# The mixer's c, v and b by seven block products in place of eight, with the state-space scan re-staged around them

## The chip, the cores and the metric

One Trainium2 chip, one of its cores. The metric is device time in microseconds (us) of one execution. Rows of the profile come from one profiled execution of the kernel before; times of runs come from three executions.

## The reference, cut to what matters

One decoder layer on x of 1024 tokens by 1024 features: a first SwiGLU feed-forward, the mixer, a second SwiGLU feed-forward, each behind an adaptive norm. The mixer is:

```python
h = modulate(rms_norm(x, mix_norm[l]), sh2, sc2)
proj = h @ w_in[l]
b_gate, c_gate, v, u = jnp.split(proj, [D_CONV, 2 * D_CONV, 3 * D_CONV], axis=-1)
y_conv = short_conv_mixer(b_gate, c_gate, v, conv_w[l])       # b * conv3_causal(c * v)
y_ssm = s5_mixer(u, ...)     # 32 groups of 16 channels, complex states scanned over time, GELU, GLU
y_mix = jnp.concatenate([rms_norm(y_conv, ...), rms_norm(y_ssm, ...)], axis=-1)
x = x + g2[:, None, :] * (y_mix @ w_out[l])
```

D_CONV is 512, so c, v and b are each a product of (1024 x 1024) by (1024 x 512), and u is a fourth of the same size.

## The kernel before, in words

**Products.** Features lie on partitions and tokens on the free axis, in two halves of 512 (`h` is 0 or 1). Every float32 operand is held as a high and a low fp32r part. `mm3` multiplies one 128-row piece of a weight tile by one 128x512 piece of an activation with three matmuls (high by high, high by low, low by high) and then calls `clock.tick()`. A projection of 128 output features over one half is eight `mm3`, 24 matmuls.

**Weights.** The class `Weights` streams raw weight tiles of 128x1024 float32 (512 KB) through three buffers by SP's DMA queue; ScalarE casts the high part (`CAST w<-raw`) and VectorE subtracts for the low part (`TENSOR_TENSOR w<-raw,w`). Four such pairs (`w`) exist at once. Where a block product needs a sum of weight blocks, GpSimd issues an accumulating DMA onto the raw tile (L175) after the earlier use of it.

**Seven products.** The feed-forwards already use `seven()` (L638): a 2x2 block product by seven instead of eight block multiplications, on combinations S1 to S4 of the activation's four blocks A11, A12, A21, A22. A group has a side "g" and a side "u"; each of its seven steps (`left`) is four `mm3` for either side, into three PSUM banks per side (A, B, C), with copies by ScalarE and sums by VectorE between. With the order `SOON` the first two steps are plain blocks of the first half, and the combinations are needed from the third step on. `combos3` (L597) makes S1 to S4 of the second feed-forward's input.

**The mixer before.** The norm h2 is followed by u: four weight tiles, 48 matmuls each for both halves, 192 in all. Its result `ya` goes to DRAM (`u_d`, 32 DMAs of 64 KB) in the scan's layout. Then, for i = 0 to 3, c_i is copied by ScalarE (`cs`), v_i is multiplied in by VectorE, and VectorE runs the three-tap convolution: one TENSOR_SCALAR and four SCALAR_TENSOR_TENSOR into `ya[i]`. Then b for both halves, multiplied into `ya`, the norm of it (`nAa`, `nAb`), the GLU (`gl`) and the output projection (`wo`). c, v and b are 12 weight tiles and 576 matmuls of 128x512.

**The scan.** It runs beside c, v and b in eight batches of four groups. `states(b)` (L1516) multiplies the input `ub` by `mi` on TensorE into `px`, copies it to `X`, sends it to `swx` with its two halves of partitions exchanged (two DMAs of 128 KB), and then on VectorE rotates (`co`, `si`), scans (four TENSOR_TENSOR_SCAN), rotates back, with a second exchange `swz`. `outputs(b)` (L1541) makes `yy` from `ub` by the Toeplitz matrix `mk` and from the states `co` by `mo`, takes the GELU (`yg`) and stores it (`y_d`). All these DMAs are issued by SP, in the order of the program.

**What sets the order.** `Clock` counts `mm3` calls; `clock.after(n, f)` runs `f` n ticks later, and each call that is due is written into the program there. A scheduler then orders each engine's instructions, and each engine executes its own in that order; a wait holds up everything behind it on the same engine. `states(b)` stands at tick 20 + 16b from the start of c, `outputs(b)` 22 ticks later (L1563, L1564). After the last batch, 32 DMAs bring `yb` back from `y_d`.

Of the kernel before, what the change touches and what calls it, by code (L numbers as in the profile page):

```python
# [21 lines left out]
P = 128  # L22
# [209 lines left out]
def hymba_layer(ctx: ExitStack, tc, x_d, xt_d, wm1_d, wmod_d, gu1_d, gs1_d, ds10_d, ds11_d, wl1_d, win_d, wout_d, glu_d, gu2_d, gs2_d, wd2_d, ds20_d, ds21_d, ds22_d, wl2_d, cols_d, cond_d, lam_d, bc_d, out_d):  # L232
# [70 lines left out]
    plain([win_d[i] for i in range(8)] + [glu_d] + [wout_d[i] for i in range(4)])  # L303
# [284 lines left out]
    lefts3 = {"S1": [], "S2": []}  # L588

    def copied3(k, h):  # L590

        left, i = {(1, 0): ("S1", 0), (1, 1): ("S1", 1), (0, 0): ("S2", 0), (0, 1): ("S2", 1)}[h, k // 4]
        if i == 0:
            lefts3[left].append(mov(f"h3{left}_{k}", dict(S1="B", S2="A")[left]))
        return lefts3[left][k % 4][:, i, :].bitcast(F32)

    def combos3(act):  # L597

        blocks.clear()
        while act[1] is None or len(act[1]) < KT:  # L600
# [3 lines left out]
        saved = scratch.tile([4, P, HALF], F32, name="s4_d")  # L604
# [7 lines left out]
        for k in range(4):  # L612
            s1, s3, s2, s4 = (t2k(f"h3w{i}_{k}")[:] for i in (1, 3, 2, 4))
            t1, t2 = (lefts3[left][k] for left in ("S1", "S2"))
# [7 lines left out]
            SP.dma_start(saved[k], s4)  # L622
            split_into("S2", t2, s2)
            yield
            split_into("S3", mov(f"h3S3_{k}"), s3)
            yield
        for k in range(4):
            t = mov(f"h3S4_{k}")
            hi, lo = t[:, 0, :], t[:, 1, :]
            SP.dma_start(lo.bitcast(F32), saved[k])  # L630
            split_into("S4", t, lo.bitcast(F32))
            yield
# [5 lines left out]
    def seven(name, between=None, kept=None, then=None, order=SEVEN):  # L638
# [11 lines left out]
        def out(side, h, fi, src, t):  # L650
            if side == "g":
# [8 lines left out]
        for n, (left, b) in enumerate(order):  # L660
            (w,) = ws.take()
            for half, side in enumerate("gu"):
# [22 lines left out]
                else:  # L685
                    if side == "g":
                        last = pools["first"].tile([P, HALF], F32, tag="first", name=f"{name}c21") if "first" in pools else acc_in_mov(f"{name}c21")
# [331 lines left out]
    u_d = scratch.tile([TAU, CH, G, J], F32, name="u_d")  # L1019
    y_d = scratch.tile([TAU, CH, G, J], F32, name="y_d")  # L1020
# [315 lines left out]
    def after1(d, h):  # L1336
        n2[h].add(x[d][h], beside=d < 6)
        if d == KT - 1:
            norm_into(act2, h, n2[h], 1, "h2")
# [20 lines left out]
    def fetch_last(left):  # L1360

        if left in ("A11", "A12", "A22"):
            i = ("A11", "A12", "A22").index(left)
            for h in range(2):
                for fi in range(2):
                    g, block = LAST[0][i], f"A{h + 1}{fi + 1}"
                    a_last[i][fi, h] = split_act(kept[g].of(block), f"fa{g}l{block}") if g else fetch(kept[g], block, "A", f"fa{g}l")

    back = [(h, k) for ks in ((0, 2), (1, 3)) for h in range(2) for k in ks]
# [5 lines left out]
    def x_back(left):  # L1375

        if left == "S4":
# [4 lines left out]
            open_x(ctx)  # L1382
# [37 lines left out]
    pools["acc"] = es2.enter_context(tc.tile_pool(name="accp", bufs=2))  # L1420
    yp = es2.enter_context(tc.tile_pool(name="yp", bufs=1))
    ya = [yp.tile([P, S], F32, tag=f"ya{i}", name=f"ya{i}") for i in range(4)]

# [6 lines left out]
    nA = [Sumsq("nAa"), Sumsq("nAb")]  # L1430
# [16 lines left out]
    def across(i, move, dram, t):  # L1447

        for g in range(8):
            move(  # L1450
                dram[:, :, 8 * i + g, :].rearrange("t c j -> c t j"), t[g * CH : (g + 1) * CH].rearrange("c (t j) -> c t j", t=TAU)
            )

    sp_open = ExitStack()
    sp = sp_open.enter_context(tc.tile_pool(name="sp", bufs=1))
    w4 = ws.take(4)
    for h in range(2):
        if h == 0:
            outs = [ps(f"u{i}_{h}") for i in range(4)]
            for k in range(KT):  # L1460
                ready(act2, h, k + 1)
                for w, o in zip(w4, outs):
                    mm3(o[:], w, k, act2[h][k], k == 0, k == KT - 1)
# [422 lines left out]
```

## Time and profile before

| what | value |
|---|---|
| three runs | 1688.48 us median, 1684.78 to 1691.4 |
| the profiled execution | 1685.48 us, of which the span from first to last instruction is 1683.7 us |
| granted TensorE clock, mean | 0.997 |
| busy: TensorE, VectorE, ScalarE, GpSimd | 98%, 64%, 41%, 10% of the span |
| u, in the span's own time | 693.8 to 741.9 us |
| c, v, b with the scan | 741.9 to 905.2 us |
| GLU, output projection | 905.2 to 937, 937 to 1040 us |

Times of rows are in us from the start of the span. A profiled execution is 1.78 us longer than its span, and this one lies 3.0 us under the median of the three runs. "PE" is TensorE's matmuls, "DVE" VectorE, "ACT" ScalarE, "POOL" GpSimd, "SPq" SP's queue of DMA issues. Busy times of neighbouring instructions overlap a little, since one starts while the last one drains.

### The profile page before, as it was taken

The numbers are of one execution on the slowest core, as the hardware profiler recorded it, in microseconds if no ns is written. First come the engines' busy times: TensorE is split into PE (matmuls) and PEld (weight loads), VectorE is DVE, ScalarE is ACT, GpSimd is POOL, SyncE is SP. The second block draws the span as 40 slices with busy tenths as digits, with TensorE's granted clock in tenths as the row PEclk, the third lists the DMA queues.
The fourth block names the chain that finished last, engine by engine and source line by source line (L and its number), as shares of the span: only waits on it lengthen the run. The fifth ranks groups of instructions, "written<-read, shape, count | busy, mean of one in ns | idle before, by whom it ended". The sixth has DMA issues, their size and how long they took to land.

```text
span 1683.7 us, 20572 instructions
## 1 busy us (share of the span) xinstructions
PE 1651.7 (98%) x7509; PEld 1360.4 (81%) x7509; DVE 1085.7 (64%) x1608; ACT 686.0 (41%) x1011; POOL 172.8 (10%) x211
## 2 busy tenths in 40 slices
PE   8999999999999999999999999999999999999998
PEld 5888888878878888788878778888888888888887
DVE  7984488869566768726556847856555555444576
ACT  6654333324455341332214416434444444322345
POOL 2010100101010102100000121000001011001004
PEclk9999999999999999999999999999999999999999
DMA  9476699989978667145653324557887777889732
GB/s 352 137 168 188 174 266 262 263 241 266 294 214 237 164 193 263 38 118 163 194 157 113 103 98 148 129 137 221 233 238 208 216 223 224 275 274 320 241 77 101
DMA packets 129272, 333.77 MB, mean 198 GB/s; under 512 B 17298, under 2 KB 41106, under 8 KB 128147
## 3 DMA queue, kind: packets, MB, share of 16 engines
q1 hardware_dynamic: 112466, 272.68, 46.7%
q0 software_dynamic: 16704, 59.78, 20.4%
q8 instruction: 59, 0.97, 0.2%
q14 instruction: 43, 0.34, 0.1%
HBM read 251.27 MB, written 72.74 MB: 192 GB/s over the span
## 4 chain that ended last, share of the span: by engine, by line
PE 83%; DVE 7%; DMA 7%; issue 2%; ACT 1%; POOL 1%; SPq 0%; DVEq 0%; POOLq 0%; ACTq 0%
PE fald L113 3%; PE fbd_1B L113 3%; PE fbd_0B L113 3%; PE p L113 3%; PE fad_0B L113 2%; PE fad_1B L113 2%; PE wo L113 2%; PE u L113 2%; PE b L113 2%; PE c L113 1%; PE fbd_1C L113 1%; PE fbd_0C L113 1%; PE v L113 1%; PE fb0d L113 1%; PE fad_0C L113 1%
## 5 line engine op out<-in xcount | busy, mean ns | idle before, releaser
L113 DVE TENSOR_TENSOR w<-raw,w 128x1024 fp32r<-128x1024 f32 (+1 forms) x247 | 298.7, 1211 | 255.1 <-ACT w L113 250.8
L113 ACT CAST w<-raw 128x1024 fp32r<-128x1024 f32 (+1 forms) x247 | 256.4, 1039 | 301.4 <-DMA raw<-in_ds 56.6
L175 POOL DMA_DIRECT2D raw<-in_gs x80 | 70.4, 883 | 737.0 <-DVE w L113 424.7
L113 DVE CUSTOM_DVE_ANT_0 wm<-wm,cact 128x1024 f32<-128x1024 f32 x56 | 76.4, 1378 | 12.9 <-DMA wm<-in_wmod 12.9
L175 POOL DMA_DIRECT2D raw<-in_ds x36 | 31.5, 875 | 312.6 <-DVE w L113 179.2
L113 PE MATMUL p<-h,w 128*128 128x512 f32 x192 | 49.4, 407 | 1.8 <-ACT h L113 1.5
L113 PE MATMUL wo<-oa,w 128*128 128x512 f32 x192 | 45.5, 391 | 2.4 <-ACT w L113 1.7
L113 PE MATMUL wo<-ob,w 128*128 128x512 f32 x192 | 45.7, 392 | 1.1 <-ACT ob L113 0.6
L113 PE MATMUL c<-h,w 128*128 128x512 f32 x192 | 46.0, 393 | 0.0
L113 PE MATMUL v<-h,w 128*128 128x512 f32 x192 | 46.0, 393 | 0.0
L113 PE MATMUL b<-h,w 128*128 128x512 f32 x192 | 45.1, 392 | 0.0
L113 PE MATMUL u<-h,w 128*128 128x512 f32 x192 | 44.8, 392 | 0.2 <-DVE h L113 0.2
L113 PEld LDWEIGHTS wo<-oa,w 128*128 128x128 f32 x192 | 35.8, 188 | 10.6 <-ACT w L113 2.1
L113 PEld LDWEIGHTS p<-h,w 128*128 128x128 f32 x192 | 35.7, 192 | 10.0 <-ACT h L113 2.0
L113 PEld LDWEIGHTS wo<-ob,w 128*128 128x128 f32 x192 | 35.7, 188 | 9.3 <-ACT ob L113 1.0
L113 PEld LDWEIGHTS u<-h,w 128*128 128x128 f32 x192 | 35.7, 188 | 8.3 <-DVE h L113 0.6
L113 PEld LDWEIGHTS b<-h,w 128*128 128x128 f32 x192 | 35.7, 188 | 7.3
L113 PEld LDWEIGHTS c<-h,w 128*128 128x128 f32 x192 | 35.5, 188 | 7.1
L113 PEld LDWEIGHTS v<-h,w 128*128 128x128 f32 x192 | 35.5, 188 | 7.1
L113 DVE TENSOR_TENSOR X<-co,X 128x512 f32<-128x512 f32 x8 | 5.5, 693 | 38.2 <-DMA swx<-X 34.6
L113 PE MATMUL fb0u<-h,w 128*128 128x512 f32 x96 | 23.8, 391 | 0.0
L113 PE MATMUL fb0g<-h,w 128*128 128x512 f32 x96 | 23.2, 389 | 0.0
(1558 smaller groups left out, 3874.9 us busy)
## 6 DMA issues: line engine op xcount, KB each, us to landing
raw<-in_gs SPq DMA_DIRECT2D x80, 512.0 KB, 4.9
raw<-in_gs POOLq DMA_DIRECT2D x80, 512.0 KB, 6.5
wm<-in_wmod SPq DMA_DIRECT2D x56, 512.0 KB, 6.2
raw<-in_ds SPq DMA_DIRECT2D x32, 512.0 KB, 4.9
raw<-in_ds POOLq DMA_DIRECT2D x32, 512.0 KB, 7.0
mw<-in_wm SPq DMA_DIRECT2D x8, 1024.0 KB, 8.7
raw<-in_win SPq DMA_DIRECT2D x16, 512.0 KB, 4.2
xb<-in_xt SPq DMA_DIRECT2D x8, 512.0 KB, 9.0
```

The source lines that it names most:

```text
L113: r = getattr(self.engine, name)(*args, **kw)
L175: self.G.dma_start(out=r, in_=src, accum_op=ALU.add)
```

## The change

c, v and b become three calls of `seven()`: `cv0` (c_0, c_1 as side g and v_0, v_1 as side u), `cv2` and `b`, all in the order `SOON`, 168 ticks in all. Their weights come as four blocks (`in_wcvb`), with 12 accumulating DMAs. `combos` makes S1 to S4 of h2, for which the norm h2 now leaves copies of its pieces (`copier`, 16 DMAs of 256 KB), and u's second half goes over four k for all four tiles first. The rows of x go to DRAM (`x_s`) and come back after the sevens. The scan is five steps per batch with 15 ticks between batches; `swx`, `swz`, `ub` and `y_d` are issued by ScalarE (`A.dma_start`); the product by `mk` is made in the first step into a PSUM tile of its own (`py`). The convolution's four taps are set two ticks apart, `yb` comes back tile by tile.

```diff
-    plain([win_d[i] for i in range(8)] + [glu_d] + [wout_d[i] for i in range(4)])
+    plain([win_d[i] for i in range(2)])
+    for i in range(3):
+        ws.seven(wcvb_d[i], soon=True)
+    plain([glu_d] + [wout_d[i] for i in range(4)])
...
-            norm_into(act2, h, n2[h], 1, "h2")
+            norm_into(act2, h, n2[h], 1, "h2", "A", copier(lefts2, "h2"))
...
+    clock.side.append(combos(act2, lefts2, "h2", "B", lambda: opened, lambda: u_free, s4_rest))
+    clock.period = 2
...
+    for k in range(4):
+        for w, o in zip(w4, outs):
+            mm3(o[:], w, k, act2[1][k], k == 0, False, more=True)
+    u_free.append(True)
...
+    def b_out(side, h, fi, src, t):
+        i = fi + 2 * (side == "u")
+        y = ya[i][:, hsl(h)]
+        joined(y, src[:], y, ALU.mult, fi == 1)
+        nA[h].add(y)
+        if nA[h].count == 4:
+            outnorm(actA, ya, nA[h], h, C_ONC, "oa", 8)
...
+    def u_load(b):
+        held["u", b] = sp.tile([P, GB, J], F32, tag="u", name=f"ub{b}", bufs=2)
+        A.dma_start(held["u", b][:], groups(u_d, b))
...
     def swapped(src, b, nm):
 
-        sw = sp.tile([P, GB * P], F32, tag="sw", name=f"{nm}{b}")
-        SP.dma_start(sw[0:64], src[64:128])
-        SP.dma_start(sw[64:128], src[0:64])
+        sw = sp.tile([P, GB * P], F32, tag=nm, name=f"{nm}{b}")
+        A.dma_start(sw[0:64], src[64:128])
+        A.dma_start(sw[64:128], src[0:64])
         return sw
...
+    def state_in(b):
+
+        u, mi, mk = (held.pop((n, b)) for n in ("u", "mi", "mk"))
         px = ps(f"px{b}")
+        py = held["py", b] = sm([P, GB * J], f"py{b}")
         for g in range(GB):
             q = slice(g * P, (g + 1) * P)
-            T.matmul(px[:, q], lhsT=held["mi"][:, q], rhs=u[:, g, :], start=True, stop=True)
+            T.matmul(px[:, q], lhsT=mi[:, q], rhs=u[:, g, :], start=True, stop=True)
+        X = held["X", b] = sp.tile([P, GB * J], F32, tag="sX", name=f"sX{b}")
+        A.copy(X[:], px[:])
+        held["sw", b] = swapped(X, b, "swx")
+        for g in range(GB):
+            q = slice(g * P, (g + 1) * P)
+            T.matmul(py[:, q], lhsT=mk[:, q], rhs=u[:, g, :], start=g == 0, stop=False, skip_group_check=True)
+        if b + 2 < NB:
+            u_load(b + 2)
...
+    STEPS = (0, state_in), (9, state_scan), (16, state_swap), (22, state_end), (27, outputs)
     for b in range(NB):
-        clock.after(20 + 16 * b, lambda b=b: states(b))
-        clock.after(20 + 16 * b + 22, lambda b=b: outputs(b))
+        for n, step in STEPS:
+            clock.after(6 + 15 * b + n, lambda b=b, step=step: step(b))
+    last = 6 + 15 * (NB - 1) + 27
     for i in range(4):
-        (w,) = ws.take()
-        cs = sp.tile([P, S], F32, tag="us", name=f"cs{i}")
+        clock.after((122, 128, 134, last + 1)[i], lambda i=i: y_back(i))
+    clock.after(last + 13, lambda: split_g(0))
+    clock.after(last + 22, lambda: split_g(1))
+    for i in range(0, 4, 2):
+        seven(f"cv{i}", order=SOON, emit=cv_out(i))
+    seven("b", order=SOON, emit=b_out)
```

**Place 1: batch 0's input product on TensorE, and ScalarE's queue ahead of it.** A number behind a name is the index of the batch, tile or weight; "x3" is one `mm3`. Before, `px0` stood behind all of c_0 and half of v_0:

```order
L113 MATMUL v0_0_6032<-h25_0_5578,w113_5865 128x512 x3
L113 MATMUL v0_0_6032<-h26_0_5586,w113_5865 128x512 x3
L113 MATMUL v0_0_6032<-h27_0_5594,w113_5865 128x512 x3
L113 MATMUL px0_6045<-ub0_5962,mi0_5956 128x128 x4
L113 MATMUL v0_1_6085<-h20_1_5706,w113_5865 128x512 x3
```

Now, on TensorE, six `mm3` after the end of u (four of `cv0gB`, then the first two rows here):

```order
L113 MATMUL cv0uB_6114<-h20_0_5546,w112_5973 128x512 x3
L113 MATMUL cv0uB_6114<-h21_0_5557,w112_5973 128x512 x3
L113 MATMUL px0_6121<-ub0_6087,mi0_6081 128x128 x4
L113 MATMUL py0_6122<-ub0_6087,mk0_6083 128x128 x4
L113 MATMUL cv0uB_6114<-h22_0_5574,w112_5973 128x512 x3
L113 MATMUL cv0uB_6114<-h23_0_5585,w112_5973 128x512 x3
L113 MATMUL cv0gA_6154<-h24_0_5596,w114_6036 128x512 x3
```

And ScalarE's queue around the end of u now, where before no DMA stood (raw70 holds the weights of w112, onto which the accumulating DMA adds before w115 is cast from it):

```order
L113 CAST w114_6036<-raw72_5641 128x1024
L113 COPY ya3_5669<-u3_1_5860 128x512
L113 CAST w115_6068<-raw70_5517 128x1024
L113 DMA ub0_6087<-u0_d_691 128x512
L113 COPY cv0gt1_6112<-cv0gB_6099 128x512
L113 COPY sX0_6127<-px0_6121 128x512
L113 DMA swx0_6129<-sX0_6127 64x512 x2
```

`px0` moved from behind 24 `mm3` to behind six, and the load of its input `ub0` stands behind a cast on ScalarE.

**Place 2: batches 1 to 4 on TensorE.** Before, the batches were spread; batch 2 began in the middle of v_1, one batch after another:

```order
L113 MATMUL v1_0_6228<-h23_0_5562,w115_5943 128x512 x3
L113 MATMUL px2_6241<-ub2_6195,mi2_6140 128x128 x4
L113 MATMUL v1_0_6228<-h24_0_5570,w115_5943 128x512 x3
L113 MATMUL v1_0_6228<-h25_0_5578,w115_5943 128x512 x3
L113 MATMUL v1_0_6228<-h26_0_5586,w115_5943 128x512 x3
```

Now, after batch 0, no matmul of the scan but the last product of batch 0 stands in `cv0`. At the end of it three batches stand together:

```order
L113 MATMUL cv0uB_6114<-h27_1_5813,w118_6255 128x512 x3
L113 MATMUL px1_6218<-ub1_6093,mi1_6138 128x128 x4
L113 MATMUL py1_6219<-ub1_6093,mk1_6140 128x128 x4
L113 MATMUL px2_6325<-ub2_6136,mi2_6235 128x128 x4
L113 MATMUL py2_6326<-ub2_6136,mk2_6237 128x128 x4
L113 MATMUL px3_6435<-ub3_6233,mi3_6342 128x128 x4
L113 MATMUL cv2gB_6488<-h20_0_5546,w119_6298 128x512 x3
```

Ten `mm3` later comes the first product that needs the states of batch 1 (`co1`):

```order
L113 MATMUL cv2gA_6547<-h24_0_5596,w121_6420 128x512 x3
L113 MATMUL cv2gA_6547<-h25_0_5606,w121_6420 128x512 x3
L113 MATMUL px4_6554<-ub4_6340,mi4_6452 128x128 x2
L113 MATMUL py1_6219<-co1_6097,mo1_6312 128x127 x4
L113 MATMUL px4_6554<-ub4_6340,mi4_6452 128x128 x2
```

The last of these products, that of batch 7, stands in the fifth of b's seven steps, 224 matmuls of 128x512 behind that of batch 1.

**Place 3: ScalarE's queue from batch to batch now.** `swz1` waits for VectorE's `si1`, the end of batch 1's scan, and the copy of batch 2 stands behind its first half:

```order
L113 CAST w122_6483<-raw74_6071 128x1024
L113 DMA swz1_6350<-si1_6095 64x512
L113 COPY sX2_6331<-px2_6325 128x512
L113 DMA swz1_6350<-si1_6095 64x512
L113 DMA swx2_6333<-sX2_6331 64x512 x2
L113 COPY cv2gt1_6513<-cv2gB_6488 128x512
L113 COPY cv2ut1_6541<-cv2uB_6515 128x512
L113 CAST w123_6543<-raw75_6196 128x1024
L113 ACTIVATE yg1_6410<-py1_6219 128x512
```

The same five lines recur for every later batch; before, ScalarE held the copies `X` and no DMA.

## Rows read from the trace of the kernel before

**Rows 1.** The page: busy time, share and instructions of each engine; the ending chain's engines.

```profile
PE 1651.7 (98%) x7509; PEld 1360.4 (81%) x7509; DVE 1085.7 (64%) x1608; ACT 686.0 (41%) x1011; POOL 172.8 (10%) x211
PE 83%; DVE 7%; DMA 7%; issue 2%; ACT 1%; POOL 1%; SPq 0%; DVEq 0%; POOLq 0%; ACTq 0%
```

**Rows 2.** Windows: length; PE, PEld, DVE, ACT, POOL busy; PEclk, DMA share, GB/s.

```profile
694.00:742.00 48.00, 46.55 (x210) 37.52 (x210) 25.84 (x37) 18.77 (x29) 3.61 (x3) 1.00 0.23 64
742.00:905.00 163.00, 156.04 (x784) 130.99 (x783) 88.78 (x143) 34.47 (x50) 1.01 (x1) 1.00 0.57 164
76.00:114.00 38.00, 38.00 (x169) 31.46 (x168) 30.49 (x67) 15.32 (x21) 4.65 (x37) 1.00 0.65 153
```

**Rows 3.** The chain of waits, 741 to 790: start, us, what.

```profile
741.88 10.88 PE c L113 x48
...
758.20 0.90 PE px L113 x8
...
759.18 0.60 ACT X L113
...
760.33 2.83 DMA swx<-X
...
787.75 1.78 PE yy L113 x16
```

**Rows 4.** The same chain, 70 to 118: the first feed-forward's group fa1, first and last of 14.

```profile
75.89 2.72 PE fa1gB L113 x12
...
111.26 2.75 PE fa1uB L113 x12
```

**Rows 5.** Waits of TensorE, 694 to 937: us in total, times, longest.

```profile
PE yy L113 <- DVE co L113: 5.3, 5, 1.6
```

**Rows 6.** Groups of VectorE instructions, 742 to 905: busy us, mean ns, idle before.

```profile
L113 DVE TENSOR_TENSOR w<-raw,w 128x1024 fp32r<-128x1024 f32 x12 | 14.6, 1218 | 14.7 <-ACT w L113 14.7
L113 DVE TENSOR_TENSOR_SCAN sz<-r,X 128x128 f32<-128x128 f32 x32 | 11.0, 405 | 0.2
L113 DVE TENSOR_TENSOR X<-co,X 128x512 f32<-128x512 f32 x8 | 5.5, 693 | 38.2 <-DMA swx<-X 34.6 <-DMA si<-si_d 3.6
L113 DVE TENSOR_TENSOR co<-co,swz 128x512 f32<-128x512 f32 x8 | 5.5, 689 | 5.4 <-DMA swz<-si 5.4
```

**Rows 7.** Transfers of swx, by tile: issue times in ns, and landing.

```profile
L113 SPq DMA_DIRECT2D swx<-X x16: 467/534/597, 759.8 to 862.6; - x16
...
DMA to landing us min/median/max: 2.5/4.6/7.1
```

**Rows 8.** The same of swz.

```profile
DMA to landing us min/median/max: 2.2/2.4/4.1
```

**Rows 9.** The same of ub.

```profile
L113 SPq DMA_DIRECT2D ub<-u_d x8: 413/430/501, 749.5 to 849.1; - x8
...
DMA to landing us min/median/max: 3.5/4.7/6.8
```

**Rows 10.** The page's DMA issues: accumulating weight transfers: count, KB, us to landing.

```profile
raw<-in_gs POOLq DMA_DIRECT2D x80, 512.0 KB, 6.5
```

**Rows 11.** VectorE in time: the norm h2's end, then the ends of batch 0's and 1's scans.

```profile
720.72 1.42 DVE L113 SCALAR_TENSOR_TENSOR h<-h2t,mods,h 128x512 fp32r<-128x512 f32 x2 [0.78 <-ACT h L113]
...
768.21 0.68 DVE L113 TENSOR_TENSOR si<-sz,si 128x512 f32<-128x512 f32 x1
...
781.41 0.69 DVE L113 TENSOR_TENSOR si<-sz,si 128x512 f32<-128x512 f32 x1
```

**Rows 12.** The combinations of the second feed-forward, by tile: ns min/median/max.

```profile
L113 ACT CAST h3S<-h3w x12: 614/620/625, 1051.9 to 1079.3; 128x512 fp32r<-128x512 f32 x12
L113 DVE TENSOR_TENSOR h3w<-h3S x4: 680/685/685, 1050.0 to 1070.8; 128x512 f32<-128x512 f32 x4
```

**Rows 13.** Windows at the only fall of the granted clock before the end.

```profile
14.00:16.00 2.00, 1.00 (x6) 0.57 (x6) 1.59 (x3) 1.97 (x4) 0.00 (x0) 1.00 1.02 414
16.00:18.00 2.00, 1.43 (x3) 0.90 (x4) 1.64 (x3) 2.00 (x3) 0.00 (x0) 0.58 1.02 416
```

More of the change, by code (lines that the diff above doesn't have):

```diff
@@ new lines, in hymba_layer @@
+    clock.period = 2
+    sp_open = ExitStack()
+    w4 = ws.take(4)
+    outs = [ps(f"u{i}_0") for i in range(4)]
+    for k in range(KT):
+        ready(act2, 0, k + 1)
+        for w, o in zip(w4, outs):
+            mm3(o[:], w, k, act2[0][k], k == 0, k == KT - 1)
+    for i in range(4):
+        A.copy(ya[i][:, hsl(0)], outs[i][:])
+    ready(act2, 1, KT)
+    x_open.close()
+    sp = sp_open.enter_context(tc.tile_pool(name="sp", bufs=1))
+    opened.append(True)
+    outs = [ps(f"u{i}_1") for i in range(4)]
@@ L1488, in v_tile, with cv_out, emit @@
-            o, s = y3[:, 0:lag, 1:], z3[:, TAU - lag :, : J - 1]
-            V.scalar_tensor_tensor(out=o, in0=s, scalar=tap[2 - lag], in1=o, op0=ALU.mult, op1=ALU.add)
+            for o, s in ((y[:, lag * J :], z[:, : S - lag * J]), (y3[:, 0:lag, 1:], z3[:, TAU - lag :, : J - 1])):
+                n += 2
+                clock.after(n, lambda lag=lag, o=o, s=s: tapped(lag, o, s))
+    def cv_out(i0):
+        c, z = {}, {}
+        def emit(side, h, fi, src, t):
+            if side == "g":
+                if t is None:
+                    t = t2k(f"c{i0}_{h}_{fi}")
+                    A.copy(t[:], src[:])
+                c[h, fi] = t
+                return
+            if fi not in z:
+                z[fi] = sp.tile([P, S], F32, tag="us", name=f"cs{i0 + fi}", bufs=2), []
+            cs, done = z[fi]
+            V.tensor_tensor(out=cs[:, hsl(h)], in0=src[:], in1=c[h, fi][:], op=ALU.mult)
+            done.append(h)
+            if len(done) == 2:
+                conv(i0 + fi, cs)
+        return emit
@@ L1558, in hymba_layer, with y_back, split_g @@
-    in_load(0)
-    out_loads(0)
-    state_loads(0)
-    state_loads(1)
+            co_load(b + 2)
+    in_loads(0)
+    mo_load(0)
+    for b in range(2):
+        u_load(b)
+        si_load(b)
+        co_load(b)
+    yb = []
+    def y_back(i):
+        yb.append(mov(f"yb{i}", dtype=F32)[:].rearrange("p a b -> p (a b)"))
+        across(i, lambda d, t: SP.dma_start(t, d), y_d, yb[i])
+    def split_g(h):
+        actG[h] = []
+        for i in range(4):
+            clock.after(2 * i, lambda i=i, h=h: actG[h].append(split_act(yb[i][:, hsl(h)], f"yg{i}_{h}")))
@@ L1588, in hymba_layer @@
-    yb = [yp2.tile([P, S], F32, tag=f"yb{i}", name=f"yb{i}") for i in range(4)]
     mods_open = ExitStack()
```

224 lines of the change are left out of this document (106 added, 118 removed).

## The prediction

> **What bounds the kernel now.** I read the page first: TensorE is busy 98% of the span, VectorE 64%, and the ending chain is 83% TensorE [rows 1]. So a shorter time must come from fewer matmuls or from the gaps between them. The windows then show where the change lies: c, v and b with the scan take 163 us, TensorE busy 156.0, VectorE 88.8, ScalarE 34.5, the DMA engines 0.57 [rows 2]. The reader is to see that VectorE, the engine that gets the new work, has 74 us free there, and that this is less than it seems: 38.2 + 5.4 us of it are waits in front of two kinds of instruction of the scan, for `swx` and `swz` [rows 6], and whatever stands behind those on VectorE waits too.
>
> The chain gives the price of the work. 48 matmuls take 10.88 us, 0.2267 us each; a batch's `px` takes 0.90 and its `yy` 1.78 [rows 3]. The stage runs from 741.9 to 905.2, 163.3 us. 576 matmuls are 130.6, eight batches 8 x 2.68 = 21.4. The norm's 16 small matmuls I put at `px`'s 0.11 us each (0.90 for eight), 1.8. What is left, 9.5 us, is waiting; 5.3 of it is `yy` behind VectorE [rows 5].
>
> **The products.** Three sevens are 3 x 168 = 504 matmuls, 72 fewer: 16.3 us. That sevens in this same order keep the rate is seen in fa1: 14 pieces of 12 matmuls at 2.72 us [rows 4], TensorE busy 38.00 of 38.00 us while VectorE works 30.49, 80% [rows 2]. If every wait of the stage went too, it would be 114.3 + 21.4 + 1.8 = 137.5 us, 25.8 less. That is the floor; the rest of the working asks which waits come back.
>
> **The combinations.** 32 VectorE operations of 0.685 us and 16 casts of 0.62 [rows 12], 22 and 10 us, run under u, where VectorE is busy 25.8 of 48 us and ScalarE 18.8 [rows 2]. That fills VectorE, 48 of 48, so the cover is just enough. They need the second half of h2, which is done at 720.7 + 1.4 = 722.1 [rows 11]. In VectorE's order 25 of them stand before the first weight of `cv0`; at 0.65 from start to start (neighbours overlap a little) that is 16.3, and with the subtraction of 1.2 [rows 6] `w112` is whole at 739.6, 2 us before u ends. I take 1 us of loss for u itself, between 0 and 2.
>
> **Batch 0 (place 1).** The accumulating DMA onto raw70 can start only then, and lands 6.5 us later [rows 10], 746.1. The cast of `w115`, which I put at the 1.2 of its VectorE half, ends at 747.3; behind it on ScalarE stands the load of `ub0`, 0.43 to issue and 4.7 to land [rows 9]: 752.4. TensorE reaches `px0` six `mm3` after u, at 741.9 + 18 x 0.2267 = 746.0. So it waits about 6 us, from 5.2 with the quickest landing of 3.5 to 8.5 with the slowest of 6.8. Before, `ub0` was issued by SP with 24 `mm3` ahead of `px0`.
>
> **Batches 1 to 7 (places 2 and 3).** This is the largest uncertain term. `cv0` holds no scan after batch 0; seven batches fall into `cv2` and b. Count from T1, the end of `cv0`. TensorE's own demand: the five small products, 4.5 us; ten `mm3`, 6.8; half of `px4`, 0.45; then the first product on `co1` at T1 + 11.7. To that on `co7` lie 224 matmuls, 50.8 us, and 14.5 small products of 0.89, 12.9: T1 + 75.4.
>
> The chain's own supply: `px1` 0.9, copy 0.6 [rows 3], two issues 1.06 [rows 7], landing L, then on VectorE two rotations, a weight, a sum, a weight, the scan, a weight and the rotation back: 4 x 0.65 + 3 x 1.15 + 1.4 = 7.4. Then `swz`, issue 0.53 and landing 2.4 [rows 8], and one sum, 0.7. From batch to batch ScalarE repeats: half of `swz`, the copy, the other half, two halves of `swx`: 0.53 + 0.6 + 0.53 + 1.06 = 2.7; then L; then VectorE's four operations and the scan, 4.0, with 1.4 of other work between them on average (weights, sums and taps standing there in the order). A period is P = 8.1 + L, and the wait of TensorE up to the last batch is 13.6 + L + 6P - 75.4.
>
> L is what the trace does not show, since no DMA is issued by ScalarE. `swx` lands in 4.6 us at the median and 2.5 at best [rows 7]; `swz`, of the same size, in 2.4 [rows 8]; the `swx` on the chain took 2.83 [rows 3]. With SP's 512 KB loads not in front of it in its queue, I take 2.8: P = 10.9, wait 6 us. With 2.5 it is 4, with 4.6 it is 19, and by what P was before, 13.2 from one scan's end to the next [rows 11], it is 22.
>
> The Trainium skill speaks against this choice: its page DMA: Bandwidth & Descriptors, section "Issuing engines are not separate DMA queues", says that DMAs started by different engines run on the same 16 DMA engines, and that issuing from several saves only the sequencer's time. By it L stays near 4.6, the wait is 19 us, and the sum below is +2 instead of -11. The same page's "Queues, rings and completion order" says that each DMA engine takes the queue rows in turn, which favours the shorter L. No row here shows a small transfer on a queue of its own.
>
> **The rest.** At the start of the GLU, VectorE must finish the last product of b, one norm piece and the first half of `yg` before the first matmul can go: three operations of 0.69, 2 us. The 48 issues on ScalarE, 25 us at 0.53, nine more weight casts and the copies of the sevens bring ScalarE to about half the stage, so it costs through its order, not its load. The raw tiles stay 12; 12 accumulating transfers of 512 KB are new, 6.3 MB; at 164 GB/s for a share of 0.57 [rows 2] the engines carry 288 GB/s, so that is 22 us of the 70 that are free. The 16 copies of h2's pieces, 4 MB or 15 us, fall before and under u, where the share is 0.23. The store and reload of x, 4 MB each, 15 us each at that rate, fall under the first feed-forward's end and under the GLU, where the transfers don't bind; without that cover they would cost those 15 us each. The taps moved apart and `yb` by tiles cost nothing while TensorE has products: the last batch has two of b's steps and the GLU's first nine `mm3`, 13 us, to come back.
>
> **The sum.** -25.8 + 6 (batch 0) + 6 (batches 1 to 7) + 2 (GLU) + 1 (u) = -10.8 us. Against the profiled execution's 1685.5 that is 1674.7; the three runs' median lies 3.0 higher, so for a median I say **1677 us**. 0.5% is 8.4 us, about what a measurement of this kernel can tell from no change, so the forecast lies little beyond it. With the bounds of its own terms (batch 0 from 5 to 8.5, batches 4 to 10, u 0 to 2) it is 1674 to 1685.
>
> **Rivals.**
> 1. Everything hides: the DMA onto raw70 comes earlier than I count, and the swaps land in 2.5 us with less between them on VectorE. -25.8 plus 2 to 6 of rest: 1664 to 1668. For it: fa1 ran without a gap at 80% of VectorE. Against: fa1 had no scan chain with round trips inside.
> 2. The queue on ScalarE does nothing for the landing: L = 4.6, P = 12.7, wait 19 us: +2, 1690. For it: the median row of `swx`, and DMA engines that carry more bytes than before. Against: `swz` landed in half the time in the same stage.
> 3. The other side: VectorE becomes the bound. The order gives it 111.6 us of work from batch 0's scan to the GLU (20 weights at 1.2, 81 operations of 0.69, 32 scans, the taps), against 88.8 before [rows 2]. It runs in order and stood idle 74.5 of 163.3 us, much of it behind `swx`. If more than 51.7 us of idling stay, the stage is no shorter; above 60 it is slower by 0.5%. That all 74.5 stay gives 186 us, +23, 1711. For it: weights are now 21 instead of 12, and a weight behind a waiting scan operation makes TensorE wait, which delays the next `px`. Against: the step of 9 ticks puts other work into the landing time, and waits for TensorE's products shrink when VectorE is late.
>
> A pause of 6 us could also cost clock: the only fall before the end came after TensorE had worked 1.00 of 2 us, from 1.00 to 0.58, between its two levels [rows 13]. Two such us lose 0.8 us; this is within the bounds above.
>
> **Chances.** The forecast 0.45, of which 0.1 ends inside 0.5%; rival 1 0.18; rival 2 0.24, of which 0.04 ends slower than by 0.5%; rival 3 0.13. Faster by over 0.5%: 0.18 + 0.35 = 0.53. Within: 0.10 + 0.20 = 0.30. Slower: 0.04 + 0.13 = 0.17. The range for 8 in 10 takes in most of rival 1 and rival 2 and leaves out the far part of rival 3: 1661 to 1694.
>
> **What would show it.** The products are right if the chain's pieces of the sevens are 2.72 us per 12. Batch 0 is right if TensorE shows one wait of 5 to 8 us at `px0`, put down to the load of `ub0`. The period is right if VectorE's `si` products of batches 1 to 7 stand about 11 us apart and TensorE waits for `co` mostly in `cv2`. L is read from the landing of `swx`. Rival 3 would show as waits of TensorE for VectorE's half of `w`. I am wrong altogether if the time moves outside 694 to 937 us of the span, as by transfers of x that hold up the first feed-forward's end.

## The result, and the profile after

| | before | after |
|---|---|---|
| median of 13 runs, us | 1686.37 (1681.13 to 1691.4) | 1694.96 (1691.4 to 1702.64) |
| profiled execution, us | 1685.48 | 1698.14 |
| last matmul of u to first of the GLU, starts, us | 741.5 to 905.2 | 742.0 to 913.3 |
| granted clock, mean | 0.997 | 0.988 |

The ratio is 1.005, 95% interval 1.0035 to 1.0065: the changed kernel is slower by about 0.5%. The forecast was 1677, the range ended at 1694, and the time lies just outside. The profiled execution of after lies 3.2 us above its median, that of before 0.9 below. Of the 12.7 us between the two, 0.5 come before u's last matmul, 7.6 between u and the GLU, and 4.4 from the GLU's start to the second feed-forward's first group (its last `fb0u` matmul starts at 1072.8 before and 1085.3 after).

The page of after, busy time and the ending chain, against [rows 1]:

```profile
PE 1648.2 (97%) x7437; PEld 1357.0 (80%) x7437; DVE 1123.0 (66%) x1667; ACT 718.1 (42%) x1064; POOL 183.9 (11%) x223
PE 80%; DMA 8%; DVE 7%; ACT 2%; issue 2%; POOL 0%; SPq 0%; ACTq 0%; DVEq 0%; POOLq 0%
```

TensorE has 72 matmuls fewer and is busy 3.5 us less, not 16.3: a lower clock stretches what is left. Taken over windows of 2 us of the whole span, its busy time multiplied by what the granted clock lacked of 1.00 sums to 14.3 us in after and 1.5 before. Its share of the chain falls from 83 to 80%.

Windows of after, u and then c, v and b with the scan, against [rows 2]:

```profile
694.00:742.00 48.00, 46.75 (x213) 38.09 (x211) 43.24 (x68) 34.00 (x58) 6.26 (x6) 1.00 0.60 188
742.20:913.30 171.10, 146.95 (x713) 123.09 (x711) 105.44 (x165) 47.51 (x67) 9.20 (x10) 0.95 0.75 196
```

Under u VectorE takes the combinations without any loss of TensorE's: from u's first matmul to its last it is 47.1 us (694.9 to 742.0) against 47.7 (693.8 to 741.5). In the stage behind it VectorE is 66 us free, as far from being the bound as before; the DMA engines have gone from 0.57 to 0.75, and the granted clock from 1.00 to 0.95.

What TensorE waits for in after, whole span, against [rows 5] (us in total, times, longest; lines of other stages left out):

```profile
PE py L113 <- DVE co L113: 12.2, 6, 3.1
PE px L113 <- DMA mi<-mi_d: 8.2, 2, 6.8
PE gl L113 <- ACT yg L113: 2.6, 1, 2.6
...
PE px L113 <- issue: 1.2, 1, 1.2
```

From u's end the stage lasts 171.1 us where the prediction's floor is 137.5, so 33.6 are lost. These four lines make 24.2. The rest is mostly clock: the same sum over windows of 2 us is 6.4 us in the stage, 3.0 in the 18 us after the GLU's start and 1.6 in a fall at 994 to 998; before, it is 0 in all three. Some 3 us of the 33.6 I can't assign.

The timeline of TensorE in after, the end of `cv0` (start, us, what, and in brackets the idle time before it and its releaser):

```profile
781.78 2.88 PE L113 MATMUL cv0uB<-h,w 128*128 128x512 f32 x12
784.50 1.05 PE L113 MATMUL px<-ub,mi 128*128 128x128 f32 x8
785.39 1.06 PE L113 MATMUL py<-ub,mk 128*128 128x128 f32 x8
793.29 2.08 PE L113 MATMUL px<-ub,mi 128*128 128x128 f32 x8 [6.84 <-DMA mi<-mi_d]
795.16 1.82 PE L113 MATMUL py<-ub,mk 128*128 128x128 f32 x8
798.33 1.13 PE L113 MATMUL px<-ub,mi 128*128 128x128 f32 x8 [1.35 <-DMA mi<-mi_d]
799.21 3.00 PE L113 MATMUL cv2gB<-h,w 128*128 128x512 f32 x12
```

This is place 2 of the change, `px1` to `px3` in a row. From `px1` to the first matmul of `cv2` it takes 14.7 us where the prediction wrote 4.5. `mi` has one buffer: its load for batch 2 can be issued only when `px1` has read the last one. SP's queue in after shows it:

```profile
766.31 8.44 SPq L113 DMA_DIRECT2D u_d<-ya  x8
774.85 0.38 SPq L113 DMA_DIRECT2D mi<-mi_d  x1
...
785.59 0.32 SPq L113 DMA_DIRECT2D mi<-mi_d  x1
```

The load for batch 1 stands behind the last of the 32 stores of u, 26 us after `px0` had left the buffer free; the next goes out right behind `px1` and lands in 7.7. The stores are not slow by themselves: before, all 32 had been issued by 749.5. Waits of SP's queue in after, 740 to 776:

```profile
SPq L113 <- DMA ub<-u_d: 7.9, 1, 7.9
SPq L113 <- DMA swz<-si: 7.7, 1, 7.7
SPq L113 <- DMA y_d<-yg: 4.8, 1, 4.8
SPq L113 <- DMA swx<-sX: 2.6, 1, 2.6
```

All four, 23.0 us, are transfers that ScalarE now issues.

Windows of after in and behind that pause, and at the start of the GLU (last three numbers: clock, DMA share, GB/s):

```profile
788.00:792.00 4.00, 0.00 (x0) 0.00 (x0) 1.41 (x3) 0.00 (x0) 0.00 (x0) 0.73 1.04 261
792.00:796.00 4.00, 2.71 (x12) 2.71 (x13) 1.79 (x3) 1.99 (x2) 0.00 (x0) 0.50 0.71 219
796.00:800.00 4.00, 2.65 (x18) 2.35 (x18) 4.00 (x8) 1.04 (x1) 0.86 (x1) 0.92 0.53 125
...
916.00:920.00 4.00, 4.00 (x12) 3.15 (x11) 2.92 (x4) 4.00 (x8) 0.00 (x0) 0.56 0.32 57
```

After 6.84 us without a matmul the clock is at its lower level, 0.50 of the upper, when TensorE starts again. After the 2.57 us at the start of the GLU it is 0.56 for 4 us of unbroken work.

Landings of `swx`, then of `swz`, in after, against [rows 7, 8]:

```profile
L113 ACTq DMA_DIRECT2D swx<-sX x16: 469/554/626, 749.5 to 872.7; - x16
DMA to landing us min/median/max: 2.4/5.6/7.6
```

```profile
DMA to landing us min/median/max: 2.4/4.9/7.0
```

ScalarE issues them now, and they land later than SP's did: `swx` in 5.6 instead of 4.6 us, `swz` in 4.9 instead of 2.4. VectorE shows the same from its side (groups, 742 to 913; before, the first of these waited 5.4 us and the second 38.2 [rows 6]):

```profile
L113 DVE TENSOR_TENSOR co<-co,swz 128x512 f32<-128x512 f32 x8 | 5.5, 690 | 25.2 <-DMA swz<-si 25.0
L113 DVE TENSOR_TENSOR sX<-co,sX 128x512 f32<-128x512 f32 x8 | 5.5, 689 | 16.4 <-DMA swx<-sX 14.1 <-DMA yb<-y_d 2.2
```

The ends of the scans of batches 1 and 7, and between them the sum with `swz1` and the first rotation of batch 2, VectorE's timeline of after:

```profile
800.69 0.68 DVE L113 TENSOR_TENSOR si<-sX,si 128x512 f32<-128x512 f32 x1
...
809.12 0.69 DVE L113 TENSOR_TENSOR co<-co,swz 128x512 f32<-128x512 f32 x1 [7.14 <-DMA swz<-si]
810.02 0.69 DVE L113 TENSOR_TENSOR sX<-co,sX 128x512 f32<-128x512 f32 x1 [0.22 <-DMA swx<-sX]
...
884.62 0.68 DVE L113 TENSOR_TENSOR si<-sX,si 128x512 f32<-128x512 f32 x1
```

Six periods take 83.9 us, 14.0 each (11.4 to 16.7), where 10.9 was predicted. In VectorE's order the sum with `swz` of one batch stands ahead of the next batch's rotation. So the landing of `swz` is a part of the period too: in these six periods VectorE waits 21.0 us for `swz`, in five of them, and then 2.3 us for `swx`, which lands little later (2.2 more in the sixth are put down to the loads of `yb`).

### The profile page after: what moved, and what is told of

Its sections match the earlier page's. It is cut to its first block, busy times and chain, and to the rows that moved or that the text cites. A ratio compares the mean times of both kernels' runs of the same rounds, so it can differ in the third digit from the quotient of the medians.

```text
span 1696.3 us, 20682 instructions
## 1 busy us (share of the span) xinstructions
PE 1648.2 (97%) x7437; PEld 1357.0 (80%) x7437; DVE 1123.0 (66%) x1667; ACT 718.1 (42%) x1064; POOL 183.9 (11%) x223
## 4 chain that ended last, share of the span: by engine, by line
PE 80%; DMA 8%; DVE 7%; ACT 2%; issue 2%; POOL 0%; SPq 0%; ACTq 0%; DVEq 0%; POOLq 0%
PE fald L113 3%; PE fbd_1B L113 3%; PE fbd_0B L113 3%; PE wo L113 3%; PE p L113 3%; PE fad_0B L113 2%; PE fad_1B L113 2%; PE u L113 2%; PE fbd_1C L113 1%; PE fbd_0C L113 1%; PE fb0d L113 1%; PE fad_1C L113 1%; PE fad_0C L113 1%; DVE w L113 1%; PE fb0u L113 1%
## 5 line engine op out<-in xcount | busy, mean ns | idle before, releaser
L113 DVE TENSOR_TENSOR w<-raw,w 128x1024 fp32r<-128x1024 f32 (+1 forms) x256 | 309.4, 1210 | 233.5 <-ACT w L113 233.1
L113 ACT CAST w<-raw 128x1024 fp32r<-128x1024 f32 (+1 forms) x256 | 265.6, 1039 | 294.6 <-DMA raw<-in_ds 59.2
L113 PEld LDWEIGHTS p<-h,w 128*128 128x128 f32 x192 | 35.1, 189 | 10.6 <-ACT h L113 2.0
L175 POOL DMA_DIRECT2D raw<-in_wcvb x12 | 10.6, 899 | 177.2 <-DVE w L113 145.9
L113 PE MATMUL gl<-yg,w 128*128 128x512 f32 x96 | 26.1, 430 | 2.6 <-ACT yg L113 2.6
L113 PEld LDWEIGHTS gl<-yg,w 128*128 128x128 f32 x96 | 19.7, 209 | 7.7 <-ACT yg L113 3.0
L113 PE MATMUL fald<-fa9lA,w 128*128 128x512 f32 x96 | 22.8, 391 | 0.0
L113 PE MATMUL fald<-fa0lA,w 128*128 128x512 f32 x96 | 22.4, 389 | 0.0
L113 PE MATMUL fald<-fa10lA,w 128*128 128x512 f32 x96 | 22.4, 389 | 0.0
L113 DVE SCALAR_TENSOR_TENSOR x<-wo,gate,x 128x512 f32<-128x512 f32 x16 | 11.4, 744 | 16.6 <-PE wo L113 16.6
```

The source lines that it names most:

```text
L113: r = getattr(self.engine, name)(*args, **kw)
L175: self.G.dma_start(out=r, in_=src, accum_op=ALU.add)
```

## The experiments

The first theory (A): one buffer for `mi` makes the three batches at the end of `cv0` wait, and the pause costs clock too. The second (B): the small exchanges land late because the DMA engines are fuller, and of what fills them the 12 accumulating transfers are new (B1). The rivals: ScalarE's queue is to blame (C), or the new staging of the scan as such (D). Later, E: the 32 stores of u hold up SP's queue and so make the cluster. A stage is given from u's last matmul to the GLU's first, starts, out of one profiled execution per kernel (171.3 us in after); a median is that of the kernel's runs.

**Two buffers (e1_mi2).**

```diff
-        held["mi", b] = ld("mi", mi_d[b], b)
-        held["mk", b] = ld("mk", mk_d[b], b)
+        held["mi", b] = ld("mi", mi_d[b], b, 2)
+        held["mk", b] = ld("mk", mk_d[b], b, 2)
...
-        if b + 1 < NB:
-            in_loads(b + 1)
+        if b + 2 < NB:
+            in_loads(b + 2)
```

> The matrices mi and mk of the scan get two buffers each, so that those of the next batch are loaded before the batch ahead of it has used its own (the GELU output yg moves to a shared tile to make room). In the changed kernel TensorE stood still 6.84 and 1.35 us at px2 and px3 for the load of mi. Theory A (the single buffer of mi, which I overlooked, makes the three batches at the end of cv0 wait for one load each): both waits vanish, the stretch from px1 to the first product of cv2 falls from 14.7 us to about 5, the clock holds there, and the time falls by 9 to 12 us against the changed kernel, to about the time before. Rival B (the round trips swx and swz set the pace of batches 1 to 7, and TensorE merely waits elsewhere): the waits for co grow by about what mi gives, and the time falls by less than 4 us.

1690.29 us, ratio 1.0021 (1.0001 to 1.0042); the stage is 162.8 instead of 171.3. Its longest wait of TensorE, 735 to 925:

```profile
PE py L113 <- DVE co L113: 13.0, 4, 6.5
```

The wait for `mi` is gone and the waits for `co` are what they were. A is a part of it and not the whole: 8.5 us of the stage in the two traces, but 4.7 us between the medians, half of the 9 to 12 that A was to give. The interval touches that of after (1.0035 to 1.0065).

**The exchanges on SP's queue (e2_sp).** `swx`, `swz`, `ub` and `y_d` go back to `SP.dma_start`, all else stays.

```diff
-        A.dma_start(sw[0:64], src[64:128])
-        A.dma_start(sw[64:128], src[0:64])
+        SP.dma_start(sw[0:64], src[64:128])
+        SP.dma_start(sw[64:128], src[0:64])
```

> swx, swz, ub and y_d are issued by SP again; all else is the changed kernel. Theory A (ScalarE's queue does nothing for the landing, 5.6 us at the median against 4.6 before, and blocks its own copies): landings stay at 4.5 to 6 us and the time stays within 4 us of the changed kernel. Rival B (the transfers on ScalarE's queue are the loss): the time falls by 5 us or more. Rival C (they are a gain, as SP's queue holds waits for free buffers in front of them): the time rises by 5 us or more.

1696.95 us, ratio 1.0075 (1.0048 to 1.0102), an interval that overlaps that of after; the stage 172.4. `swx` lands in 3.7 us, `swz` in 5.8. The queue neither gains nor costs what could be measured, taken as a whole, and C falls. It does change where TensorE waits: on SP alone the stores of u are out by 760.5, the batches stand apart and `mi` costs 0.5 us, but `co` costs 14.0, `ub` 3.5 and the clock 9.1.

**The exchanges left out (e3_noswap, e5_mi2_noswap).** ScalarE copies the tile instead; e5 has the two buffers as well.

```diff
-        A.dma_start(sw[0:64], src[64:128])
-        A.dma_start(sw[64:128], src[0:64])
+        A.copy(sw[:], src[:])
```

> The exchange of the two halves of partitions is left out: swx and swz are plain copies by ScalarE, so the scan's result is another; all other work stays. This takes away 32 transfers of 128 KB with their round trips. Theory B (landings of 5 to 7 us set the pace): the waits of TensorE for co, 12.2 us, fall to under 2 and the time falls by 14 us or more, clock included. Theory A (mi is the larger part): the 8 us at px2 and px3 stay, and the time falls by less than 14 us.

> Both suspects gone at once: two buffers for mi and mk, and the exchange left out as before (swx and swz are plain copies by ScalarE, so the scan's result is another). The sevens, the combinations, the weights and all other transfers stay. From the last matmul of u to the first of the GLU the changed kernel takes 171.3 us, with two buffers 162.8, without the exchange 155.3. If the two causes are separate and complete, the stretch comes down to about 145 (137.5 of work, 3 at the GLU, a few for the clock) and the profiled time to about 1670. If something else holds TensorE (VectorE's load, late weights, late u_d), it stays above 152.

One run each: 1684.34 and 1676.01 us, stages of 155.3 and 153.9. No wait for `co` is left in e3, and 6.3 us for `mi`; its time is 13.8 below the profiled execution of after and 10.6 below the median, where B asked for 14. e5 missed what I expected by 9 us of stage. Its waits, 735 to 925:

```profile
PE px L113 <- DMA ub<-u_d: 3.4, 1, 3.4
PE gl L113 <- ACT yg L113: 2.6, 1, 2.6
PE py L113 <- DVE co L113: 2.5, 1, 2.5
PE py L113 <- ACT yg L113: 2.3, 2, 1.2
```

Even with no round trip in the scan, five short waits of 10.8 us together stay, and about 3 us of clock (the same sum as above).

**The old staging under the sevens (e4_oldscan).** The scan's steps stand together on SP's queue again, with the product by `mk` late.

```diff
-    STEPS = (0, state_in), (9, state_scan), (16, state_swap), (22, state_end), (27, outputs)
+    STEPS = (0, state_in), (0, state_scan), (0, state_swap), (0, state_end), (22, outputs)
...
-            clock.after(6 + 15 * b + n, lambda b=b, step=step: step(b))
+            clock.after(20 + 16 * b + n, lambda b=b, step=step: step(b))
```

> The sevens stay and the scan is staged as before: all of a batch's input, scan and swaps at one place from tick 20 with 16 ticks between batches, the product by mk beside that by mo 22 ticks later, all transfers by SP. Theory A (sevens are sound, the new staging lost their gain by putting three batches together): no such cluster, the stage takes about 150 us and the time falls to 1672 to 1682. Rival D (c, v and b are too short now for eight batches of about 13 us each however they are staged): TensorE waits for co at almost every batch, and the time stays at 1690 or above.

1706.73 us, ratio 1.0137 (1.0105 to 1.0168). Much of its 177.8 us of stage is one wait of 16.1 for the last batch's `mk`, whose load I had set behind the outputs of the batch before. That wait is this variant's own, so it bounds nothing closely; it shows no sign that the old staging would have been better, and it doesn't settle D.

**No accumulating transfers (e6_noadd, e11_mi2_noadd).**

```diff
-        ws.seven(wcvb_d[i], soon=True)
+        ws.seven(wcvb_d[i], soon=True, adds=False)
```

> The changed kernel without the 12 accumulating transfers onto the weights (so the sevens multiply other weights; the count of products, casts and loads is the same). It takes 6.3 MB out of a stage in which the DMA engines are busy 0.75 of the time. Theory B1 (the swaps land late, 5.6 and 4.9 us at the median, because the engines are full): both medians fall below 4 us and the time falls by 5 us or more. Rival (they land late because of what is in front of them on ScalarE's own queue or for their form): medians stay above 4.5.

> The sevens with two buffers for mi and mk and without the 12 accumulating transfers (so they multiply other weights). Each alone took the profiled time from 1698 to 1687 and 1678. If both act through the same waits (loads and swaps late on full DMA engines), the two together give little more than the larger: 1672 to 1679. If they are separate: 1667 or below, and the landings of swx and swz stay near 3.4 and 2.4 us.

One run each: 1677.83 and 1676.46 us, stages of 155.2 and 152.0. e6's waits, then its landing of `swx` and of `swz`:

```profile
PE py L113 <- DVE co L113: 4.0, 3, 3.0
PE gl L113 <- ACT yg L113: 2.6, 1, 2.6
PE px L113 <- DMA mi<-mi_d: 2.6, 2, 1.9
```

```profile
DMA to landing us min/median/max: 2.2/3.4/6.8
```

```profile
DMA to landing us min/median/max: 2.2/2.4/6.8
```

B1 came as expected: without the 12 transfers of 512 KB, 6.3 MB, the stage is 16 us shorter, `swx` lands in 3.4 us instead of 5.6 and `swz` in 2.4 instead of 4.9. The wait for `mi` shrinks with them from 8.2 to 2.6, so the second buffer of e11 adds little, as expected if both act through the same waits.

Of the two landings it is that of `swz` which goes with these transfers in every run. Its median is 3.7 to 5.8 us in the six kernels that have them and the exchanges (after, e1, e2, e4, e12, e13; DMA share of the stage 0.69 to 0.76), and 2.3 to 2.8 in the nine without (before, e6, e7, e8, e10, e11, e14, e15, e16; 0.56 to 0.63). That of `swx` doesn't divide so: 3.7 to 5.6 with them, 3.0 to 6.0 without. Another path from these transfers to the scan is ScalarE's queue: in after a cast waits there 6.8 us for an accumulated tile, until 792.98, and in e6 no cast does. But the chain that ended last runs beside it, through the landing of `swx1` (786.72 to 794.09).

**Eight plain products under the new staging (e7_plain, e8_plain_mi2, e10_plain_py).** No sevens, no combinations, no accumulating transfers; e8 adds the two buffers, e10 gives `py` a PSUM bank of the products' kind. In e7 a half of b enters the result with the other sign.

```diff
-        ws.seven(wcvb_d[i], soon=True)
+        for q in (0, 3, 1, 2):
+            ws.plain(wcvb_d[i][q])
...
-        seven(f"cv{i}", order=SOON, emit=cv_out(i))
-    seven("b", order=SOON, emit=b_out)
+        eight(f"cv{i}", cv_out(i))
+    eight("b", b_out)
```

> The new staging of the scan with plain products: c, v and b are made from the same four blocks by eight block products in place of seven (576 matmuls), without combinations, without accumulating transfers and without the copies of h2; everything else is the changed kernel, mi with one buffer. In its order on TensorE the batches stand 12 to 14 mm3 apart with no cluster. Theory A (the new staging is sound by itself, but in the sevens the first loads come late and the batches crowd together): no wait at px beyond 2 us, the stretch from u to the GLU takes 153.8 of work plus 3 to 6, and the time falls to 1676 to 1682, below the kernel before. Rival D (the staging itself, with transfers on ScalarE, costs): the time is at or above the kernel before.

> The plain products of the run before, now with two buffers for mi and mk, so that batch 1's mi is loaded before the 32 stores of u_d instead of behind them on SP; b's signs are set right. In the run with plain products TensorE stood 11.5 us at px1 for that load and ran at half clock for some 8 us after it. Theory A (the new staging is sound once the first loads are early): that stall and the low clock go, the stretch from u to the GLU comes from 173.7 to 157 us, and the time falls to 1678 to 1684, below the kernel before. Rival D (transfers on ScalarE or the staging cost by themselves): it stays at 1690 or above.

> The same, with py in the six PSUM banks of the products in place of the two of its own, which eight block products leave free. TensorE waited 4.9 us in four places for the GELU of an older batch to release py. If those waits are only for the bank: 2 to 5 us less than with py apart. If the GELU is late because ScalarE's queue is blocked behind swz: no change beyond 1.5 us.

1699.41 (ratio 1.0092, 1.007 to 1.0114), 1697.0 (1.0052, 1.0035 to 1.0069) and 1690.97 us (1.0024, 1.001 to 1.0037). The first two missed by 13 us and more; e10 is 6.0 below e8, a little more than expected. `swz` lands fast there (2.3 to 2.4 us, `swx` 3.9 to 4.2) and nothing waits for `co`; in place of that TensorE has one long wait, `px1` in e7 (11.5 us) and `px2` in e8 (8.9). SP's queue in e8 names it:

```profile
777.04 6.95 SPq L113 DMA_DIRECT2D u_d<-ya  x8
784.08 0.37 SPq L113 DMA_DIRECT2D mi<-mi_d  x1
```

The loads stand behind the stores of u, more than 30 us after u has ended. That is where theory E comes from. Here too SP's queue waits for ScalarE's transfers meanwhile (`swx` 8.6, `swz` 8.4, `ub` 6.8, `y_d` 3.3 us, 740 to 786).

**u in four stores (e13_wide1, e12_wide).** 4 DMAs of 512 KB in place of 32 of 64 KB; the rows of `mi` and `mk` are permuted to suit. e12 has the two buffers besides.

```diff
-        across(i, lambda d, t: SP.dma_start(d, t), u_d, ya[i])
+        SP.dma_start(u_d[i][:].rearrange("g c t j -> (g c) (t j)"), ya[i][:])
```

> The changed kernel with u stored in four transfers of 512 KB in place of 32 of 64 KB (u_d keeps ya's order; ub is loaded with its partitions in the order channel, step, and the rows of mi and mk are put in that order, so the result is the same). mi and mk keep one buffer. The traces showed SP busy issuing those 32 stores until 775 us, with stops behind transfers of other queues, and mi, mk of batch 1 and later behind them. In the new order on TensorE the batches stand 18 rows apart and none together. Theory E (the stores of u hold SP's queue, so the first loads of the scan come late and the batches crowd into cv2): no wait at px over 2 us, the waits for co fall below 6 us in all, the stretch from u to the GLU falls from 171.3 to about 150 us, and the time falls to 1674 to 1682, below the kernel before. Rival B (full DMA engines and late swaps set the pace wherever the batches stand): waits for co stay above 10 us and the time stays above 1686.

> The same with two buffers for mi and mk as in the first experiment. Theory E: once the batches stand apart one buffer is enough, and this is within 3 us of the run with one. Theory A (the single buffer is a cause of its own): 4 to 8 us faster than that run.

1688.28 us both, ratios 1.0024 (1.0014 to 1.0035) and 1.0009 (0.9995 to 1.0023), stages of 161.4 and 162.5. SP's queue in e13:

```profile
734.55 8.48 SPq L113 DMA_DIRECT2D u_d<-ya  x4
751.58 0.57 SPq L113 DMA_DIRECT2D mi<-mi_d  x1
...
765.09 0.56 SPq L113 DMA_DIRECT2D mi<-mi_d  x1
```

The loads of `mi` come 13 to 18 us apart from 751.6 on, no two batches stand together, and one buffer is enough. E is right about the cluster, yet the time missed what I expected by 6 to 14 us and stays above 1686, as rival B had it: `swx` still lands in 4.8 us and `swz` in 4.1, and TensorE's longest waits are

```profile
PE py L113 <- DVE co L113: 6.1, 2, 3.1
PE px L113 <- DMA ub<-u_d: 4.2, 1, 4.2
```

By the medians e13 is 6.7 us faster than after, by their ratios to the kernel before 4.4, and not the 9.9 of the two traces' stages.

**Both causes away, and the stores alone (e14_wide_noadd, e15_plain_py_wide, e16_before_wide).** These join the edits above: e14 is e13 without accumulating transfers, e15 is e10 with four stores, e16 the kernel before with four stores.

> u in four stores as in e13_wide1, and the sevens of c, v and b without the 12 accumulating transfers (they multiply other weights, so the result is another). If the cluster of batches and the accumulating transfers are two separate causes, their parts add up: e13 took 14.8 us off the changed kernel's profiled time, e6 took 20.2; some of both is the same wait (the one for mi was still 2.6 in e6), so 1664 to 1670 and a stage of 146 to 150 us. If they are one and the same lateness, 1673 to 1678, about what e6 gave alone. A stage over 150 in any case would say that about 10 us of it are neither: the granted clock, the last wait of b and the GLU's start.

> The new staging of the scan with eight plain block products (no accumulating transfers, no combinations), py in the products' banks, two buffers for mi and mk, and u in four stores. If the stores of u are what held up the second batch there too (8.6 us at px2 in e10_plain_py, profiled 1692.6), that wait goes and the stage falls from 164.7 to about 156: 1681 to 1685 profiled, 2 to 4 us below the kernel before. If something else holds px2 (the reload of x, the load of ub), the wait moves and the time stays within 1688 to 1693.

> The kernel before with u in four stores instead of 32 and nothing else changed. There TensorE has 24 mm3 between u and px0 and waits only 5.3 us in all, for co, so the stores stand under other work: within 3 us of the kernel before, 1682 to 1687. If the 32 stores also delay the loads of batches 1 and 2 on SP there, up to 5 us faster.

e14: one run of 1673.52 us, a stage of 153.8. Its u began at 690.7, 3.3 us earlier than in e6, ahead of the stage; counted from u's start, the GLU starts 1.5 us earlier than in e6. So as far as one execution each can tell, the two causes don't add up. (The expectation's 14.8 us for e13 is 12.7 by the profiled times.) TensorE waits in e14 5.8 us for `co`, 3.2 for an older batch's GELU and 2.6 at the GLU.

e15: 1684.26 us, ratio 0.9989 (0.9973 to 1.0005). The wait at `px2` is gone, the stage is 159.8, and its clock is 1.00 throughout. So the new staging by itself, with two buffers and its first loads early, costs nothing that could be measured, and D falls as well. e16: 1687.52, ratio 1.002 (1.0004 to 1.0036), so the stores of u hold up nothing in the kernel before; four larger ones are no gain there. No version that gives the full result is measurably faster than the kernel before.

The stage in us, by the two causes, from one profiled execution each:

| | with accumulating transfers | without |
|---|---|---|
| the changed kernel | 171.3 | 155.2 |
| batches apart (two buffers / four stores) | 162.8 / 161.4 | 152.0 / 153.8 |

## Why the prediction was wrong

The forecast had 14 us lost in the stage (6 + 6 + 2) over the floor of 137.5; 33.6 were.

- **The products: right.** All full pieces of the sevens in the chain up to 784 take 2.72 to 2.74 us per 12 matmuls, as [rows 4]. The 16.3 us are saved, and then lost again. For example:

```profile
753.84 2.72 PE cv0uA L113 x12
```

- **u and its combinations: right in place, with no loss instead of 1 us.** u takes 47.1 us against 47.7 before, and VectorE is busy 43.2 of 48 us.
- **Batch 0: too dear.** `px0` waited 1.2 us, not 6: ScalarE issued the load of `ub0` at 743.9 and not at 747.3, since the accumulated tile that the cast ahead of it needs was there at 743.7 and not at 746.1. And the profile puts the wait down to `issue`, and not to that load, as the prediction expected.
- **Batches 1 to 7: wrong, and this decides it.** The step that failed is the landing in the round trip. L, that of `swx`, was taken as 2.8 us "with SP's 512 KB loads not in front of it"; it was 5.6. That of `swz` was taken from [rows 8] as 2.4 and stood outside the period; it was 4.9, and VectorE's order puts it inside, with 21.0 us of waiting in the six periods. L = 5.6 in the prediction's own formula gives a period of 13.7 (measured 14.0) and a wait of 13.6 + 5.6 + 82.2 - 75.4 = 26.0. Found were 12.2 for `co`, 8.2 for `mi` and 6.4 of clock, 26.8. That these agree so closely is in part luck, since the formula knows neither the late `swz` nor the waits for `mi` nor the clock. Behind the late landings stands a step that was priced at nothing: the 12 accumulating transfers were held to be free because "the engines carry 288 GB/s", so that they fit. They fit, and without them the stage is 16 us shorter in e6. That the queue on ScalarE would shorten L is shown wrong: `swx` landed in 5.6 us there, in 4.6 on SP before and in 3.7 on SP in e2. The Trainium skill's page DMA: Bandwidth & Descriptors, section "Issuing engines are not separate DMA queues", says that issuing from several engines saves only the sequencer's time. This trace agrees in that the landing got no shorter, but it also got longer than the 4.6 by which the prediction priced that rule.
- **"The five small products, 4.5 us": wrong, 14.7.** I had quoted the order in which `px1`, `px2` and `px3` stand together and not asked where three loads into one buffer come from. The late load of `mi1` behind them is a price of ScalarE's queue that was not asked for either: SP's stores of u waited 23.0 us for transfers that ScalarE issues. e1 and e13 are worth 8.5 to 9.9 us of stage by this, 4 to 7 by the medians; without the accumulating transfers the same edits are worth 1.4 to 3.2. That both are one lateness seen in two places (where TensorE waits at `mi`, the chain of the scan catches up, and it waits less at `co`) fits these numbers and is not shown by itself.
- **The clock: 0.8 us was too little.** Priced at one fall, it was 6.4 us in the stage, in falls behind the waits of 6.8, 3.1, 2.7 and 2.1 us, and 3.0 behind that of 2.6 at the GLU's start. This is also why the GLU's term was 2.6 + 4.4 instead of 2.
- **The rivals.** Rival 2 had the mechanism (DMA engines that carry more, a late `swx`) and nearly the time, 1690, but with L still too short. Rival 3's sign did not come: TensorE's list has no wait for `w` in the stage, and `w` waited for ScalarE 6.0 us in all, against 14.7 before. Its sum did: VectorE stood idle 66 us, above the 60 that it named, 39.1 of them for the two exchanges.

The formula is no full account. In e5, with no transfer in the round trip, it leaves no wait, and the stage was still 16.4 over its floor: 2.6 at the GLU, 3.4 at `ub`, 4.8 at `py`, about 3 of clock, and smaller ones. Whether short waits cause one another through the clock or stand alone was not tried. Nor is it shown how an accumulating transfer delays a small one more than a plain load of its size does: no run put plain loads in its place.

## What to carry to other kernels

Price a new large transfer by what it delays and not by the free share of the DMA engines: where a chain has a round trip through small transfers per batch, multiply the longer landing by the number of batches, and read from the waiting engine's order which of the transfers stand in the round trip. When an order puts several batches next to each other, look for the buffer that they share and the queue that refills it. And where TensorE is near 100% busy, count clock on top of the longer waits: in after those of 2.1 to 6.8 us in the stage were followed by falls of 6.4 us in all. It is no fixed price: in the kernel before, TensorE waited 2.6 us for `bl` at 360 to 363 us and the granted clock stayed at 1.00, and in after it waited 2.2 us at the same place and the clock fell to 0.50.

## What was not expected of the hardware

SP's queue, which was to be relieved, waited longer for the exchanges after they had been moved to ScalarE. Waits of SP's queue in after, 700 to 912, and in the kernel before, 700 to 905:

```profile
SPq L113 <- DMA swz<-si: 41.7, 9, 8.2
```

```profile
SPq L113 <- DMA swz<-si: 9.0, 5, 2.9
```

So moving a transfer to another engine's queue didn't take it out of the way of the first queue's: SP still waits for it to land, now 41.7 us. In e13 this is 24.4, with 28 transfers fewer on SP. Some 27 us of the 41.7 are the kernel's own doing and no matter of the hardware: the load of `si` for the batch after next goes into the buffer that `swz` reads, and five of these loads are issued within 0.2 us of its landing. 13.9 more are one wait of 7.7 us among the stores of u and one of 6.2 among the loads of `yb`, which share no buffer with `swz`; what ties them to it is not shown.
